# Six modulation steps of a hybrid attention block move from stage B to ahead of stage A, and their weights land in the heads' hl and pt tiles

## The chip, the core and the metric

The kernel runs on one core of one Trainium2 chip. The metric is device time in microseconds (us) of one execution, taken as the median of several runs. A core has five engines that run their own instruction streams and wait for each other through semaphores: PE (matrix multiply; its weight loads are listed as PEld), DVE (vector), ACT (scalar functions), POOL (general purpose) and SP, which here only starts DMA transfers. Each stream is in order: an instruction that waits holds up all that stand behind it on its engine. That holds for SP too, so a transfer whose buffer is not yet free keeps the later ones back.

## What is computed

The reference is a block of two layers on 512 latent tokens and 256 context tokens of width 1024. Cut to what matters:

```python
for l in range(2):
    sh, sc, gt = split(silu(c) @ w_ada[l] + b_ada[l], 3)              # and the same for c_ctx
    h  = rms_norm(x,   norm_g[l]) * (1 + sc)   + sh
    hc = rms_norm(ctx, norm_g[l]) * (1 + sc_c) + sh_c
    qa, ka, va, ga, qb, kb, vb, gb, qn, kn, vn, gn = split_proj(h @ w_in[l])     # and for hc
    ya = differential attention (4 heads, two softmaxes each)  * silu(ga)        # group A
    yb = grouped-query attention (6 heads, 2 key/value heads)  * silu(gb)        # group B
    yn = neighbourhood attention (6 heads, window, bias)       * silu(gn)        # group C
    y  = concatenate([ya, yb, yn]) @ w_out[l]
    x  = x + gt * y                                    # and ctx, in the first layer
```

The first line is the *modulation*: a product of two vectors with a matrix of 1024 x 3072 per layer. It gives a shift, a scale and an output gate for each of the 1024 features.

## The kernel before, in words

**Layout.** Activations lie with features on the 128 partitions. The input projection is cut into chunks of columns (`CH`): a0 and a1 hold keys, values and queries of group A, b0 and b1 those of B, c0, c1 and c2 those of C, and ga, gb, gn the gates. A chunk is 256 or 384 columns wide and is worked through in six tiles of 128 tokens (four of the latent stream, two of the context). A tile is 24 matmuls into one bank of PSUM: eight slices of features, three products each (the operands are split into a high and a low part, `mm3`, lines 679 to 681). Its weights come as raw float32 tiles by SP (line 76) and are split by ACT (line 89) and DVE or POOL (line 92). A raw buffer, of which there are three, is free for the next load when line 92 is done.

**Modulation.** The matrix is worked through in blocks of 128 columns, 24 per layer. One block is 512 KB, loaded in two halves of 256 KB. A *step* (`ada_step`, the generator `ada_blocks`) does one block: it starts the two loads of the block after it (line 227), does eight matmuls of 32 columns for its own (line 241; the profile counts sixteen, as each is two passes), copies the result on DVE (line 246), sums four strips with a selector matmul (line 248), and adds bias on DVE (line 251 or 254). The first call only loads. Blocks that layer 0 needs at its start are done earlier by `ada_pair` (line 204); the generator's list holds 32 more: the eight gate blocks of layer 0, sixteen of layer 1, and the eight gate blocks of layer 1.

**Order of the work.** After the a0 chunk (`proj_first`), seven calls of `ada_step` follow. Then come, layer by layer, the chunks a1 and ga (`F1`), stage A (heads of group A with the chunks b0, b1 and gb), stage B (heads of B with c0, c1, c2 and gn) and stage C. Within `proj` a step is put after every n-th tile; n is the cadence `st["cad"]`, set from the table `AK`: entry 0 is the number of steps right after a0, entry 1 the cadence in a1 and ga, entry 2 that in stage A (0: none), entry 3 that in stage B. In layer 0, a1 and ga have twelve tiles and stage B's chunks 24. This is the order in which the program is written; a scheduler then moves each instruction by priority (`prio` shifts it), by when its inputs are ready in its own model of time, and by when a buffer of the pool is free. So the instructions on an engine can stand in another order than in the code, and the steps right after a0 are spread over the tiles of a1.

**Buffers.** Tiles of one tag share a number of buffers; a new tile waits until the last reader of the one before it in that buffer is done. The tags here are `adw` (2 buffers of 2 KB per partition, for modulation weights), `hl` and `pt` (4 buffers of 3 KB each). In the stages of heads, `hl` takes the float16 high and low parts of a head's probabilities (ACT line 861, POOL line 862), and SP's transposing transfer (line 864) writes them to `pt`, from which PE does the pv matmuls (lines 897 and 898). Each is used for other things at other times: the modulation weights of the opening (`ada_load`), the six copies of a0's keys that are normalized and rotated (`qk_evac` with a tag; the last reader is DVE, line 506), and the part sums at the end of a layer. A step ahead of stage A takes its PSUM bank from `psV`, which the pv matmuls also use; a step in stage B takes it from `psP`, the two banks of the projection tiles.

The step takes its tile in these lines:

```python
def load(l, b):
    ts = []
    for r in range(2):
        t = sb([128, 512], F32, "adw", 2).rearrange("p (k n) -> p k n", n=128)
        SP.dma_start(out=t, in_=w_ada[l, b, :, 4 * r:4 * r + 4, :])
        ts.append(t)
    return ts
```

Of the kernel before, what the change touches and what calls it, by code (L numbers as in the profile page):

```python
# [10 lines left out]
F32 = mybir.dt.float32  # L11
# [30 lines left out]
}  # L42
REST = {"C": 7}
AK = [[6, 2, 0, 2], [0, 1, 0, 2]]
VSHARE = {"HA": (0, 1), "H": (0, 1), "G": (1, 1), "T": (1, 4), "HC": (1, 8), "WB": (1, 2), "WC": (1, 1),
          "W1": (1, 1)}

# [69 lines left out]
def tile_hybrid_block(ctx: ExitStack, tc: tile.TileContext, xT_d, cT_d, ng_d, w_ada, bT_d, w_in, w_out,  # L117
# [9 lines left out]
    share = Share(nc)  # L127

    def sb(shape, dt=F32, tag="", bufs=1):
        return pool.tile(shape, dt, tag=tag, bufs=bufs, name=tag)  # L130

    def prio(off):
        def deco(f):
            def g(*a, **k):
                tc.cur_priority += off
                try:
                    return f(*a, **k)
                finally:
                    tc.cur_priority -= off
            return g  # L140
        return deco
# [37 lines left out]
    def new_mods(l):  # L179
        mods[l] = (sb([128, KT, 2], F32, "mA", 2), sb([128, KT, 2], F32, "mB", 2), sb([128, KT, 2], F32, "mG", 2))  # L180
# [39 lines left out]
    def ada_blocks(blocks):  # L220


        def load(l, b):
            ts = []
            for r in range(2):
                t = sb([128, 512], F32, "adw", 2).rearrange("p (k n) -> p k n", n=128)
                SP.dma_start(out=t, in_=w_ada[l, b, :, 4 * r:4 * r + 4, :])
                ts.append(t)
            return ts

        nxt = load(*blocks[0])
        yield
        for i, (l, b) in enumerate(blocks):
            if l not in mods:
                new_mods(l)
            ts = nxt
            ps = (psV if share.phase == "1" else psP).tile([128, 512], F32, tag="pv" if share.phase == "1" else "p",
                                                           name="ada")
            for r in range(2):
                for g in range(4):  # L240
                    PE.matmul(ps[32 * g:32 * g + 32, 0:128], lhsT=cS[:, 4 * r + g, :], rhs=ts[r][:, g, :],
                              start=(r == 0), stop=(r == 1), tile_position=(0, 32 * g))
            if i + 1 < len(blocks):
                nxt = prio(-100)(load)(*blocks[i + 1])
            t = sb([128, 128], F32, "adt", 1)
            V.tensor_copy(t, ps[:, 0:128])
            src = ps[:, 128:130]
            PE.matmul(src, lhsT=t, rhs=sel, start=True, stop=True)
            w, kt = divmod(b, 8)
            if w == 1:  # L250
                V.tensor_scalar(out=mods[l][0][:, kt, :], in0=src, scalar1=bT1[:, l, kt:kt + 1],
                                scalar2=ng[:, l, kt:kt + 1], op0=ALU.add, op1=ALU.mult)
            else:
                V.tensor_scalar(out=mods[l][1 if w == 0 else 2][:, kt, :], in0=src, scalar1=bT[:, l, b:b + 1],
                                scalar2=None, op0=ALU.add)
            yield

    def ada_step():
        st["done"] = st.get("done", -1) + 1
        next(st["ada"], None)  # L260
# [22 lines left out]
    for l in range(DEPTH):  # L283
        for c in ORDER:
            n, c0 = CH[c][1], sum(v[1] for k, v in CH.items() if k < c)
# [747 lines left out]
    def run(gen):  # L1033
        for _ in gen:
            pass
# [5 lines left out]
    def fill(l, toks):  # L1041
        for c in toks:
            if c in CH:
                yield from proj(l, [c])
            elif c == "y":
                n = 6 if l == 0 else 4
                for j in range(0, n, 2):
                    y_pair(l, j)
                    yield
                    yield  # L1050
                for j in range(n):
                    if (l, "B", j) not in turned:
                        y_build(l, "gb", j)
                    yield
            elif c == "n":
                for db in range(KT):
                    while any((l, "C", j) not in turned for j in range(3)):
                        yield
                    out_head(l, db)
                    yield  # L1060
            else:
                yield from out_parts(l)
# [141 lines left out]
    if True:  # L1204
# [47 lines left out]
        proj_first(0, "a0", [[0, 1, 2, 3, 4, 5]], before0)  # L1252
        for _ in range(AK[0][0] + 1):
            ada_step()
        for l in range(DEPTH):
            share.phase = "1"
            st["cad"] = AK[l][1]
            run(fill(l, F1))
            st["cad"] = AK[l][2]
            both(l, "A", FA)  # L1260
            st["cad"] = AK[l][3]
            both(l, "B", FB)
# [108 lines left out]
```

## Time and profile before

| | us |
|---|---|
| median of 3 runs | 922.99 (919.12 to 923.62) |
| the profiled execution, its own time | 921.41 |
| its span in the trace | 919.6 |
| PE / DVE / ACT / POOL busy in the span | 824.1 / 681.9 / 593.1 / 544.1 |
| mean granted clock of PE | 0.957 |

The profile is one execution, recorded instruction by instruction. A row of the timeline gives start and length in us, the engine, the source line, the operation with the tiles it writes and reads, and in brackets the idle time of the engine ahead of it with what ended that. A row of the list of waits names who waited for whom, with the total in us, the number of times and the longest. A row of the stage table gives a stretch of time, its length, and for each engine the busy time with the number of instructions; behind them stand the granted clock of PE (1.00 is full speed), the mean share of the DMA engines that was busy, and GB/s.

### The profile page before, as it was taken

The numbers are of one execution on the slowest core, as the hardware profiler recorded it, in microseconds if no ns is written. First come the engines' busy times: TensorE is split into PE (matmuls) and PEld (weight loads), VectorE is DVE, ScalarE is ACT, GpSimd is POOL, SyncE is SP. The second block draws the span as 40 slices with busy tenths as digits, with TensorE's granted clock in tenths as the row PEclk, the third lists the DMA queues.
The fourth block names the chain that finished last, engine by engine and source line by source line (L and its number), as shares of the span: only waits on it lengthen the run. The fifth ranks groups of instructions, "written<-read, shape, count | busy, mean of one in ns | idle before, by whom it ended". The sixth has DMA issues, their size and how long they took to land. (4 is left out here: it accounts for less than half of the span.)

```text
span 919.6 us, 17947 instructions
## 1 busy us (share of the span) xinstructions
PE 824.1 (90%) x6386; PEld 705.7 (77%) x6386; DVE 681.9 (74%) x1306; ACT 593.1 (64%) x1269; POOL 544.1 (59%) x503
## 2 busy tenths in 40 slices
PE   6898988896998899896999989989959999987988
PEld 3687877795987688784778879978848878875667
DVE  4985787988778866557755798789977976876743
ACT  5334577785887687577663445478758888878630
POOL 1638855899698565434421036939988886654310
PEclk9999998998999999998999989999979999998999
DMA  9924895645879997998798723784547789999642
GB/s 325 320 88 127 202 198 151 139 102 136 190 156 212 223 213 178 223 262 217 145 232 245 246 76 92 173 206 98 123 131 188 133 199 255 205 233 250 129 87 88
DMA packets 307193, 165.46 MB, mean 180 GB/s; under 512 B 256544, under 2 KB 275232, under 8 KB 306976
## 3 DMA queue, kind: packets, MB, share of 16 engines
q1 hardware_dynamic: 307104, 164.33, 74.5%
q8 instruction: 50, 0.82, 0.4%
q14 instruction: 39, 0.32, 0.1%
HBM read 86.55 MB, written 15.47 MB: 111 GB/s over the span
## 5 line engine op out<-in xcount | busy, mean ns | idle before, releaser
L862 POOL TENSOR_TENSOR hl<-p,hl 128x768 f16<-128x768 f32 (+3 forms) x138 | 205.4, 1492 | 170.7 <-ACT hl L861 159.0
L679 PE MATMUL proj<-whi,bigL 128*128 128x384 f32 (+1 forms) x592 | 203.0, 344 | 8.5 <-DVE tb L602 5.1
L680 PE MATMUL proj<-wlo,bigL 128*128 128x384 f32 (+1 forms) x592 | 199.6, 337 | 0.8 <-POOL wlo L92 0.7
L681 PE MATMUL proj<-whi,bigL 128*128 128x384 f32 (+1 forms) x592 | 196.7, 334 | 0.0
L841 ACT ACTIVATE p<-sc,nb,gsc 128x768 f32<-128x768 f32 (+3 forms) x200 | 166.3, 845 | 10.9 <-DVE p L857 4.6
L827 DVE TENSOR_REDUCE mx<-sc 128x1 f32<-128x768 f32 (+2 forms) x128 | 118.6, 931 | 30.3 <-PE sc L775 30.3
L861 ACT CAST hl<-p 128x768 f16<-128x768 f32 (+3 forms) x144 | 104.4, 725 | 46.4 <-DMA pt<-hl 29.9
L679 PEld LDWEIGHTS proj<-whi,bigL 128*128 128x128 f32 x592 | 115.0, 194 | 18.9 <-DVE tb L602 7.2
L680 PEld LDWEIGHTS proj<-wlo,bigL 128*128 128x128 f32 x592 | 115.6, 195 | 3.9 <-POOL wlo L92 1.5
L681 PEld LDWEIGHTS proj<-whi,bigL 128*128 128x128 f32 x592 | 114.5, 194 | 2.7 <-issue 1.6
L92 POOL TENSOR_TENSOR wlo<-raw,whi 128x768 fp32r<-128x768 f32 (+1 forms) x44 | 82.8, 1889 | 31.7 <-ACT whi L89 28.1
L89 ACT CAST whi<-raw 128x768 fp32r<-128x768 f32 (+1 forms) x104 | 80.1, 779 | 25.3 <-DMA raw<-in_w_in_dram 11.1
L897 PEld LDWEIGHTS <-pt 128*128 128x128 f16 x736 | 66.4, 100 | 36.8 <-DMA pt<-hl 23.2
L679 PE MATMUL proj<-whi,bigC 128*128 128x384 f32 (+2 forms) x224 | 75.6, 337 | 1.0 <-ACT xn L462 1.0
L92 DVE TENSOR_TENSOR wlo<-raw,whi 128x768 fp32r<-128x768 f32 (+1 forms) x60 | 61.5, 1028 | 19.4 <-ACT whi L89 18.1
L680 PE MATMUL proj<-wlo,bigC 128*128 128x384 f32 (+2 forms) x224 | 74.3, 332 | 0.0
L163 POOL TENSOR_TENSOR rsqb<-rsqb,half 128x12 f32<-128x12 f32 (+2 forms) x25 | 68.5, 2739 | 9.7 <-DVE rsqb L162 8.8
L681 PE MATMUL proj<-whi,bigC 128*128 128x384 f32 (+2 forms) x224 | 73.6, 331 | 0.0
L898 PEld LDWEIGHTS <-pt 128*128 128x128 f16 x736 | 66.8, 100 | 4.6 <-issue 2.4
L775 PE MATMUL sc<-bigL 128*128 128x512 f16 (+4 forms) x184 | 46.5, 314 | 18.5 <-ACT p L841 18.1
L897 PE MATMUL pv<-vA,pt 128*128 128x128 f16 (+2 forms) x424 | 52.1, 230 | 12.1 <-DMA pt<-hl 12.1
L829 ACT ACTIVATE nb<-mx,lnp,gsc 128x1 f32<-128x1 f32 (+1 forms) x104 | 39.9, 385 | 33.3 <-DVE mx L827 22.5
(327 smaller groups left out, 2038.6 us busy)
## 6 DMA issues: line engine op xcount, KB each, us to landing
raw<-in_w_in_dram SPq DMA_DIRECT2D x64, 384.0 KB, 3.9
adw<-in_w_ada_dram SPq DMA_DIRECT2D x68, 256.0 KB, 3.5
raw<-in_w_out_dram SPq DMA_DIRECT2D x16, 384.0 KB, 4.5
raw<-in_w_in_dram SPq DMA_DIRECT2D x16, 256.0 KB, 3.0
g_d<-tb SPq DMA_DIRECT2D x20, 192.0 KB, 2.8
gt<-g_d SPq DMA_DIRECT2D x18, 192.0 KB, 3.6
hl<-in_w_ada_dram SPq DMA_DIRECT2D x12, 256.0 KB, 4.8
pt<-in_w_ada_dram SPq DMA_DIRECT2D x12, 256.0 KB, 4.9
```

The costliest lines, as they stand in the source:

```text
L89: self.nc.scalar.copy(out=hi, in_=raw2)
L92: self.share("W").tensor_tensor(out=lo, in0=raw2, in1=hi.bitcast(F32), op=ALU.subtract)
L163: G.tensor_tensor(out=y, in0=x, in1=half[:, 0:n], op=ALU.pow)
L679: PE.matmul(ps, lhsT=xh, rhs=hi, start=(kt == 0), stop=False)
L680: PE.matmul(ps, lhsT=xh, rhs=lo, start=False, stop=False)
L681: PE.matmul(ps, lhsT=xl, rhs=hi, start=False, stop=(kt == KT - 1))
L827: V.tensor_reduce(out=mx[:, 0:ns], in_=ps[:, 0:w * ns].rearrange("p (a b) -> p a b", b=w), axis=AX.X, op=ALU.max)
L841: A.activation(out=p[:, w * x:w * x + w], in_=u["ps", i][:, w * x:w * x + w], func=AF.Exp, bias=u["nb", i][:, x:x + 1], scale=lc[l]["sc"][ ...
L861: A.copy(out=hl[:, 0:n], in_=p)
L862: lo_eng.tensor_tensor(out=hl[:, n:2 * n], in0=p, in1=hl[:, 0:n], op=ALU.subtract)
L897: PE.matmul(po[r, :], lhsT=pt[:, b, r], rhs=V_[:, vt, c0:129], start=first, stop=False)
L898: PE.matmul(po[r, 0:65 - c0], lhsT=pt[:, nb + b, r], rhs=V_[:, vt, c0:65], start=False, stop=stop)
```

## The change

Two edits. The table `AK` for layer 0 goes from a step after every second tile of a1 and ga to one after every tile, and in stage B from every second tile to every fourth. So twelve steps in place of six are written into a1 and ga, and six in place of twelve into stage B; with the six after a0, 18 blocks in place of twelve are done ahead of stage A. The total stays. And while `share.phase` is "1", that is in the calls after a0 and in a1 and ga of both layers, a step's two halves are loaded into an `hl` and a `pt` tile in place of two `adw` tiles. In stage B they still go to `adw`. Layer 1's eight steps keep their place, and their loads move to the other tags with the same edit.

```diff
-AK = [[6, 2, 0, 2], [0, 1, 0, 2]]
+AK = [[6, 1, 0, 4], [0, 1, 0, 2]]
...
         def load(l, b):
             ts = []
             for r in range(2):
-                t = sb([128, 512], F32, "adw", 2).rearrange("p (k n) -> p k n", n=128)
+                if share.phase == "1":
+
+                    t = sb([128, 768], F32, *(("pt", 4) if r else ("hl", 4)))[:, 0:512]
+                else:
+                    t = sb([128, 512], F32, "adw", 2)
+                t = t.rearrange("p (k n) -> p k n", n=128)
                 SP.dma_start(out=t, in_=w_ada[l, b, :, 4 * r:4 * r + 4, :])
                 ts.append(t)
             return ts
```

Lines behind the edit are five higher in the changed kernel (227 becomes 232, 241 becomes 246, 679 becomes 684, 897 becomes 902). As each step loads for the one after it, the nineteenth block of the list is loaded ahead of stage A and used by the first step of stage B.

How the instructions move is read from the built programs. First SP's queue from the last raw loads of a0 to the first transposes of A's keys (`raw` are projection weights, `stg` the finished keys). Before:

```order
L76 DMA raw<-in_w_in_dram 128x768 x2
L227 DMA adw<-in_w_ada_dram 128x512 x2
L76 DMA raw<-in_w_in_dram 128x512 x4
L227 DMA adw<-in_w_ada_dram 128x512 x2
L76 DMA raw<-in_w_in_dram 128x512
L227 DMA adw<-in_w_ada_dram 128x512 x5
L534 DMA_TRANSPOSE bigL<-stg 128x8x128 x2
```

Changed:

```order
L76 DMA raw<-in_w_in_dram 128x768 x2
L232 DMA adw<-in_w_ada_dram 128x512 x2
L76 DMA raw<-in_w_in_dram 128x512 x5
L232 DMA pt<-in_w_ada_dram 128x512
L232 DMA hl<-in_w_ada_dram 128x512 x2
L232 DMA pt<-in_w_ada_dram 128x512
L232 DMA hl<-in_w_ada_dram 128x512
L232 DMA pt<-in_w_ada_dram 128x512 x2
L232 DMA hl<-in_w_ada_dram 128x512
L539 DMA_TRANSPOSE bigL<-stg 128x8x128 x2
```

The early `adw` pair carries the generator's first block before the change; now it carries stage B's first one that goes to `adw`, and the generator's first block is loaded into `hl` and `pt` behind the fifth raw load. The third step's pt half and the fourth's hl half go into buffers that a0's first two copies leave.

Second, PE at the end of a0 (`projs` and `proj` are projection banks, `cS` the two modulation vectors, `adt` the copy, `sel` the selector, `vb` a small sum for the scale of the values). Before:

```order
L680 MATMUL projs<-wlo,bigC 128x384
L681 MATMUL projs<-whi,bigC 128x384
L241 MATMUL ada<-adw,cS 32x128 x8
L248 MATMUL ada<-sel,adt 128x2
L241 MATMUL ada<-adw,cS 32x128 x4
L679 MATMUL proj<-whi,bigL 128x384
L680 MATMUL proj<-wlo,bigL 128x384
```

Changed, where the first step stands, 24 matmuls (one tile of a1) later:

```order
L685 MATMUL proj<-wlo,bigL 128x384
L686 MATMUL proj<-whi,bigL 128x384
L546 MATMUL vb<-vna_405,ones 128x1
L246 MATMUL ada<-hl,cS 32x128 x4
L246 MATMUL ada<-pt,cS 32x128 x4
L684 MATMUL proj<-whi,bigL 128x384
L685 MATMUL proj<-wlo,bigL 128x384
```

The first step moved behind the first tile of a1. The second stands 24 projection matmuls behind it, and the third 27 behind the second.

Third, PE at the first pv matmul, the first reader of a finished head (`sc` are scores). Before:

```order
L679 MATMUL proj<-whi,bigL 128x256
L680 MATMUL proj<-wlo,bigL 128x256
L681 MATMUL proj<-whi,bigL 128x256
L679 MATMUL proj<-whi,bigL 128x256
L897 LDWEIGHTS pt
L897 MATMUL pv<-vA,pt 128x128
```

Changed:

```order
L685 MATMUL proj<-wlo,bigC 128x256
L780 LDWEIGHTS bigL
L780 MATMUL sc<-bigL 128x512
L780 LDWEIGHTS bigL
L780 MATMUL sc<-bigC,bigL 128x256
L686 MATMUL proj<-whi,bigC 128x256
L902 LDWEIGHTS pt
L902 MATMUL pv<-vA,pt 128x128
```

Both stand behind 18 score matmuls. Ahead of it were 163 projection matmuls of width 256 (all of ga and 19 of b0) and the matmuls of twelve steps; now it is 264 of width 256 (ga and five tiles of b0) and the matmuls of 18 steps.

## The prediction

> **What bounds the kernel now.** I read the page's busy shares first, then the busy time by stage, then who PE waited for in the stages that the change touches, and last the rows of PE, SP and DVE around those waits.
>
> ```profile
> span 919.6 us, 17947 instructions
> PE 824.1 (90%) x6386; PEld 705.7 (77%) x6386; DVE 681.9 (74%) x1306; ACT 593.1 (64%) x1269; POOL 544.1 (59%) x503
> ```
>
> PE is busy for 90% of the span, so about 95 us of PE idle are all that a change without new arithmetic can win. The next rows split the part that matters here: the chunks a1 and ga ahead of stage A (from the end of a0 to the first pv matmul), layer 0's stage A, its stage B, and the like stretch of layer 1.
>
> ```profile
> 68.60:139.40 70.80, 64.88 (x542) 54.76 (x541) 51.32 (x122) 41.23 (x105) 50.36 (x49) 0.96 0.79 180
> 139.40:254.30 114.90, 100.37 (x727) 90.12 (x725) 96.74 (x147) 86.29 (x217) 93.46 (x96) 0.95 0.62 139
> 254.30:413.30 159.00, 149.28 (x1243) 128.11 (x1244) 110.17 (x218) 117.62 (x221) 97.22 (x72) 0.98 0.92 211
> 574.70:606.00 31.30, 30.02 (x285) 26.68 (x283) 23.17 (x47) 14.56 (x34) 27.69 (x27) 1.00 0.80 182
> ```
>
> After length, the columns are busy PE, PEld, DVE, ACT and POOL, each with its count, then granted clock, DMA share, GB/s. Stage B is PE's: 149.3 of 159.0 us. Stage A is shared: PE idles 14.5 us while DVE and POOL are busy for 97 and 93 of 115. Ahead of stage A PE idles 5.9 us, and the list of PE's waits between 62 and 140 us says for what: almost only for modulation weights.
>
> ```profile
> PE ada L241 <- DMA adw<-in_w_ada_dram: 5.4, 5, 2.0
> PE ada L248 <- DVE adt L246: 0.4, 1, 0.4
> ```
>
> PE's rows place two of these five waits; the clock was halved soon after both:
>
> ```profile
> 72.01 0.43 PE L241 MATMUL ada<-adw,cS 128*32 128x128 f32 x8 [1.97 <-DMA adw<-in_w_ada_dram]
> 135.96 0.43 PE L241 MATMUL ada<-adw,cS 128*32 128x128 f32 x8 [1.67 <-DMA adw<-in_w_ada_dram]
> 73.00:76.20 3.20, 3.20 (x12) 3.20 (x12) 1.88 (x6) 1.83 (x6) 3.20 (x5) 0.50 0.25 89
> 138.00:140.70 2.70, 2.70 (x15) 2.61 (x14) 1.09 (x3) 2.09 (x4) 0.73 (x1) 0.50 1.08 391
> ```
>
> At a granted clock of 0.50, 3.2 us of matmuls do the work of 1.6, and 2.7 us that of 1.4. So the two waits cost 3.0 us beyond themselves.
>
> The Trainium skill (TensorE: Matmul & The Clock Gate, Part 1: The HAM clock gate) says that the clock drops after an idle window of about 3.4 us. By that rule waits of 2 us would cost no clock; the trace disagrees, with 0.50 after 1.97 and after 1.67 us. With no clock loss in the terms below, the sum would be -3.0 in place of -4.4, and the time 920.0.
>
> **The change part by part.** *What a step costs PE.* A step puts two groups of ada matmuls and one selector pair between projection matmuls:
>
> ```profile
> 81.04 0.34 PE L681 MATMUL proj<-whi,bigL 128*128 128x384 f32 x1
> 83.12 0.34 PE L681 MATMUL proj<-whi,bigL 128*128 128x384 f32 x1
> 83.30 0.34 PE L679 MATMUL proj<-whi,bigL 128*128 128x384 f32 x1
> 83.56 0.43 PE L241 MATMUL ada<-adw,cS 128*32 128x128 f32 x8
> 83.92 0.45 PE L680 MATMUL proj<-wlo,bigL 128*128 128x384 f32 x1
> 87.18 0.34 PE L680 MATMUL proj<-wlo,bigL 128*128 128x384 f32 x1
> 87.36 0.28 PE L248 MATMUL ada<-sel,adt 128*128 128x2 f32 x2
> 87.50 0.42 PE L681 MATMUL proj<-whi,bigL 128*128 128x384 f32 x1
> ```
>
> Twelve projection matmuls start 2.08 us apart (81.04 to 83.12), 0.173 each. With a group between them the next starts 0.62 later, so a group costs 0.45; the selector pair makes 0.32 of 0.17, so 0.15. One step is 2 x 0.45 + 0.15 = 1.05 us. Six moved steps are 6.3 us of PE that go from stage B to the stretch ahead of A: nothing by themselves, as PE is the busy engine in both.
>
> *What goes ahead of stage A (layer 0).* With up to four tile pairs in place of one, a load is issued up to three steps ahead of its use, and the later steps find their weights there. I take all 5.8 us of waits and the 3.0 us of halved clock as gone: -8.8.
>
> *What comes in their place.* The first of these loads is now queued behind the fifth raw load of chunk a1, and until the six a0 copies in the hl and pt tiles are finished only one pair is free. The rows that set this:
>
> ```profile
> 68.34 0.34 PE L681 MATMUL projs<-whi,bigC 128*128 128x384 f32 x1
> 69.53 0.68 DVE L92 TENSOR_TENSOR wlo<-raw,whi 128x512 fp32r<-128x512 f32 x1
> 70.23 0.33 SPq L76 DMA_DIRECT2D raw<-in_w_in_dram  x1
> 84.27 0.68 DVE L506 TENSOR_TENSOR stg<-pt,stg 128x512 f16<-128x512 f32 x1
> L227 SPq DMA_DIRECT2D adw<-in_w_ada_dram x24: 327/372/1086, 69.1 to 137.1; - x24
> DMA to landing us min/median/max: 2.4/3.5/6.0
> ```
>
> The raw load starts when the split L92 has freed its buffer (70.21). The two ada loads follow at 70.56 and 70.93 (0.37 to issue one); the second lands 3.5 us on, at 74.4. PE ends a0 at 68.5, does one tile (24 x 0.173 = 4.2) and the small vb pair (0.2) and is there at 72.9: it waits 1.5. The second step's loads go out at about 75.1 into the same pair and are there by 79.0; PE comes at 79.4: no wait. The third step's pt tile is the one that L506 releases at 84.95, so its load lands at 88.4, and PE is there at about 84.6: it waits 3.8. From then on the copies release a tile every few microseconds and the lead grows. I take 5.3 us of waits, and one halved clock of 1.6, as after the 1.97: +6.9. The bounds are 1.5 (the release comes earlier; 3.8 and 1.6 vanish) and 13.5 (both loads take the longest landing, 6.0, so 2.5 more each, and both cost the clock).
>
> *Stage B loses six of its twelve steps.* There a step holds one of the two projection banks until DVE has copied and added, and PE waited at steps as follows (254 to 440 us):
>
> ```profile
> PE yt L640 <- DVE mB L254: 2.4, 1, 2.4
> PE ada L248 <- DVE adt L246: 1.7, 1, 1.7
> PE ada L248 <- DVE vnc L539: 1.5, 1, 1.5
> ```
>
> That is 5.6 us at twelve steps; half of it goes, -2.8, with bounds 0 and -5.6.
>
> *Layer 1's eight steps* also load into hl and pt now. PE's one wait there, between 573 and 612 us, goes: -0.7. Their number and place in the code stay.
>
> ```profile
> PE ada L241 <- DMA adw<-in_w_ada_dram: 0.7, 1, 0.7
> ```
>
> *The heads start later.* The cast of the first head needs an hl tile, which the last modulation loads now hold. Before, the first pv matmul came here:
>
> ```profile
> 117.27 0.28 PE L680 MATMUL proj<-wlo,bigL 128*128 128x256 f32 x1
> 117.63 0.28 PE L680 MATMUL proj<-wlo,bigL 128*128 128x256 f32 x1
> 139.44 0.33 PE L897 MATMUL pv<-vA,pt 128*128 128x128 f16 x1
> ```
>
> By the order of the built program, 163 matmuls of width 256 and 12 steps stand ahead of it before, 264 and 18 after, with 18 score matmuls in both. The 101 more cost 0.12 us each (0.36 for three), 11.9, and the steps 6.3: PE is 18.2 us of work ahead when the first pv comes, and that is 18.2 less the 1.9 us won (8.8 - 6.9), 16.3 us later: 155.7. Stages A and B then have the same heads and 18.2 us less of PE's other work. PE was 94% busy in B, DVE and ACT 69 and 74%; I take it that nearly all comes back and 1.0 us is lost in new waits for heads. The bounds are 0 and 18.2.
>
> *The held pair.* The nineteenth block is loaded ahead of stage A and used at B's first step, so one hl and one pt tile are out through stage A. ACT's waits for its cast into hl between 140 and 255 us (first row), and between 255 and 440 (second):
>
> ```profile
> ACT hl L861 <- DVE p L857: 8.7, 6, 4.3
> ACT hl L861 <- DMA pt<-hl: 8.3, 7, 3.6
> ```
>
> In A the cast never waited for a tile, in B it did for 8.3 us with four. I take 0 for three in A; the bound is 8.3 of ACT, in a stage where ACT has 29 us to spare.
>
> *Sum:* -8.8 + 6.9 - 2.8 - 0.7 + 1.0 = -4.4. The profiled execution took 921.4 us, 1.8 more than its span; -4.4 makes 917.0 of it. It lies 1.6 below the median of the runs, 923.0, so the median becomes 918.6. About 0.5%, 4.6 us, is what a measurement of this kernel can tell from no change, so the forecast is a gain at the edge of that.
>
> **The rivals.** *A larger gain:* the copy of a0 that the third step's load waits for is finished 4 us earlier, and the 3.8 and 1.6 fall away: -9.8, 913.2. For it: a built order in which the third step stands after only two tiles. Against: the copy goes through POOL first, which is busy throughout 77 to 82 us (the fifth column).
>
> ```profile
> 77.00:82.00 5.00, 5.00 (x42) 4.34 (x42) 2.38 (x13) 0.85 (x3) 5.00 (x6) 1.00 0.33 105
> ```
>
> *Nothing to measure:* both opening waits cost the clock (+1.6), and stage B's waits were DVE's lateness that the remaining steps meet as before (0 for -2.8): -4.4 + 1.6 + 2.8 = 0.0, 923.0. For it: the three waits at steps in B are single ones of twelve.
>
> *Slower:* from the first pv on, the heads are the bound. They start 16.3 us later, and the 18.2 us taken from PE come back only as far as DVE, ACT and POOL can run the heads faster. With two thirds lost, 12.1 for 1.0, the sum is +6.7: 929.7. It decides from 5.4 us lost on (slower than before) and shows from 10.0. For it: stage A's PE idle of 14.5 us, with DVE and POOL above 80%. Against: stage B, where PE is the one that is full, is longer.
>
> **How the numbers follow.** Forecast 0.40, its own range 915.5 to 921.5; larger gain 0.20; nothing 0.20; slower 0.20. Nearly half of the forecast, nearly all of the larger gain and some spread from the rest lie past -4.6 us: faster 0.41. Slower by more than 4.6: most of the slower case and a little of the others, 0.20. Within: 0.39. The range reaches from stage B's full 5.6 us on top of the larger gain, less some (908), to just past the slower case (931).
>
> **What would show it.** Right: no wait of PE for hl or pt loads after the fourth step ahead of A, one or two before it (72 to 75 and 85 to 89 us), granted clock of 1 near 138; the first pv at 155.7 (153 to 158); stage B's steps down to six and B shorter by 15 us or more. Wrong: PE waiting for ada loads all along the stretch; a first pv past 160; PE's waits for the heads' exp (L841) and their transposes growing by more than 6 us in A and B, which would be the slower case; ACT waiting for hl in stage A, which would be the held pair.

## The result, and the profile after

The changed kernel takes 931.55 us (median of 4 runs, 929.76 to 936.03); the kernel before, in runs on the same chip, 921.92. The medians differ by 9.6 us; the ratio over the runs (here and below it is an estimate of its own, not the quotient of the medians) is 1.0123, with a 95% interval of 1.0100 to 1.0147: slower, where 918.6 was forecast. The profiled execution took 929.76, 8.35 more than that of before.

The page of the changed kernel, first two lines:

```profile
span 928.0 us, 17959 instructions
PE 826.9 (89%) x6386; PEld 708.5 (76%) x6386; DVE 673.8 (73%) x1306; ACT 593.4 (64%) x1269; POOL 547.2 (59%) x503
```

PE's work is the same; its idle time and its halved clock grew. To see where, both traces are cut at the same pieces of work: at the start of the 145th, 433rd, 865th, 1440th and 1441st projection matmul. These are the end of a0; of a1 and ga; of b0, b1 and gb; of stage B's chunks; and the first of layer 1. Before, then the changed kernel (columns as in the stage table of the prediction):

```profile
72.40:133.00 60.60, 58.97 (x481) 50.36 (x478) 41.96 (x100) 34.21 (x88) 46.37 (x43) 0.97 0.77 176
133.00:244.90 111.90, 95.46 (x707) 85.06 (x705) 97.58 (x148) 81.71 (x200) 87.54 (x88) 0.94 0.62 136
244.90:413.00 168.10, 158.38 (x1299) 136.66 (x1298) 115.41 (x228) 125.35 (x244) 105.39 (x82) 0.98 0.92 212
413.00:535.40 122.40, 109.64 (x819) 88.14 (x819) 85.42 (x193) 66.17 (x142) 31.70 (x39) 0.95 0.84 215
535.40:919.60 384.20, 345.71 (x2595) 301.20 (x2595) 286.71 (x493) 254.76 (x525) 243.08 (x211) 0.95 0.69 156
```

```profile
70.60:131.80 61.20, 61.19 (x518) 53.73 (x519) 41.41 (x106) 32.53 (x84) 43.18 (x44) 0.97 0.89 222
131.80:237.60 105.80, 94.09 (x736) 82.59 (x735) 84.92 (x141) 72.79 (x169) 81.12 (x79) 0.98 0.62 147
237.60:414.70 177.10, 159.78 (x1264) 137.97 (x1262) 127.61 (x232) 137.74 (x281) 115.85 (x92) 0.96 0.81 184
414.70:542.00 127.30, 110.22 (x809) 89.66 (x808) 89.01 (x198) 67.68 (x146) 34.68 (x39) 0.92 0.82 211
542.00:928.00 386.00, 347.24 (x2595) 301.55 (x2595) 276.84 (x493) 253.31 (x525) 244.83 (x211) 0.95 0.68 156
```

The stretches differ by -1.8 (up to the 145th), +0.6, -6.1, +9.0, +4.9 and +1.8 us: 8.4 in all. At the end of stage A's chunks, the 865th projection matmul, the changed kernel is 7.3 us ahead, with six modulation steps more behind it and 48 pv matmuls fewer; stage B takes 9.0 back; the rest of layer 0 and layer 1 lose 6.7 more.

**Ahead of stage A the change did what it says.** PE's waits between 62 and 155 us, all of them:

```profile
PE proj L684 <- ACT pt L467: 2.1, 1, 2.1
PE proj L684 <- DVE vnb L547: 0.8, 1, 0.8
```

No wait for modulation weights is left, not even at the start. PE's rows show why, and where the first pv came:

```profile
70.61 0.45 PE L684 MATMUL proj<-whi,bigL 128*128 128x384 f32 x1 [2.15 <-ACT pt L467]
76.66 0.43 PE L246 MATMUL ada<-hl,cS 128*32 128x128 f32 x8
155.48 0.23 PE L902 MATMUL pv<-vA,pt 128*128 128x128 f16 x1
```

PE first waits 2.15 us for an a0 copy to leave its bank and then works at half clock (below), so it comes to the first step at 76.66; its weights had been there.

**The heads' first cast** is the row to look at next. ACT's rows before and after:

```profile
118.48 0.82 ACT L861 CAST hl<-p 128x768 f16<-128x768 f32 x1
```

```profile
144.68 0.83 ACT L866 CAST hl<-p 128x768 f16<-128x768 f32 x1 [0.56 <-PE ada L246]
```

It comes 26.2 us later, and what released it is the matmul of a modulation step: the four hl tiles were full of weights. ACT itself idles only 0.56 us for it; the rest of the delay lies in what stands ahead of the cast in ACT's order. The heads do not catch up: the 24th cast, counted in order of time, is still 22.8 us late. Before, then changed:

```profile
261.79 0.39 ACT L861 CAST hl<-p 128x256 f16<-128x256 f32 x1
```

```profile
284.64 0.41 ACT L866 CAST hl<-p 128x256 f16<-128x256 f32 x1
```

**In stage B** the heads of group A are still being finished. PE's waits between 248 and 415 us, the first three:

```profile
PE pv L902 <- DMA pt<-hl: 5.2, 5, 1.3
PE proj L684 <- DVE mB L259: 3.4, 1, 3.4
PE proj L684 <- DVE vA L591: 3.1, 1, 3.1
```

PE waits 3.45 us for a projection bank that a step holds, and DVE's rows show what stood ahead of the step's last operation (L259): the end of a head of group A (L929, which itself waited for POOL).

```profile
272.01 0.38 PE L253 MATMUL ada<-sel,adt 128*128 128x2 f32 x2 [0.66 <-DVE adt L251]
275.85 0.69 PE L684 MATMUL proj<-whi,bigL 128*128 128x384 f32 x1 [3.45 <-DVE mB L259]
```

```profile
272.34 0.68 DVE L832 TENSOR_REDUCE mx<-sc 128x2 f32<-128x512 f32 x1
273.60 2.00 DVE L929 TENSOR_TENSOR o<-tA,rA 128x256 f32<-128x256 f32 x1 [0.57 <-POOL rA L926]
275.52 0.14 DVE L544 TENSOR_REDUCE vnc<-vnc 128x1 f32<-128x4 f32 x1
275.59 0.20 DVE L259 TENSOR_SCALAR mB<-ada,bT 128x2 f32<-128x2 f32 x1
```

Both such waits came with a halved clock, as did the one at 70.6 (the stage table over those stretches):

```profile
272.50:279.30 6.80, 3.45 (x11) 3.46 (x12) 6.23 (x9) 6.47 (x18) 5.84 (x6) 0.51 0.59 149
293.00:299.80 6.80, 4.68 (x15) 4.69 (x16) 2.91 (x6) 4.96 (x8) 5.80 (x8) 0.51 0.99 211
71.10:74.50 3.40, 3.40 (x12) 3.40 (x12) 3.28 (x9) 3.18 (x12) 3.40 (x7) 0.51 0.65 222
```

**After stage B**, between 415 and 542 us, PE's longest waits are of other kinds, two of them for the heads' outputs that are turned (`yt`) for the output projection (`op`):

```profile
PE yt L645 <- DVE bigL L649: 3.9, 1, 3.9
...
PE op L1102 <- DVE bigL L628: 2.6, 1, 2.6
```

### The profile page after: what moved, and what is told of

It is laid out like the page before. It is cut to its first block, busy times and chain, and to the rows that moved or that the text cites. A ratio compares the mean times of both kernels' runs of the same rounds, so it can differ in the third digit from the quotient of the medians.

```text
span 928.0 us, 17959 instructions
## 1 busy us (share of the span) xinstructions
PE 826.9 (89%) x6386; PEld 708.5 (76%) x6386; DVE 673.8 (73%) x1306; ACT 593.4 (64%) x1269; POOL 547.2 (59%) x503
## 5 line engine op out<-in xcount | busy, mean ns | idle before, releaser
L867 POOL TENSOR_TENSOR hl<-p,hl 128x768 f16<-128x768 f32 (+3 forms) x138 | 207.8, 1510 | 157.3 <-ACT hl L866 147.9
L846 ACT ACTIVATE p<-sc,nb,gsc 128x768 f32<-128x768 f32 (+3 forms) x200 | 166.7, 844 | 27.3 <-POOL hl L867 12.1
L832 DVE TENSOR_REDUCE mx<-sc 128x1 f32<-128x768 f32 (+2 forms) x128 | 118.7, 930 | 29.0 <-PE sc L780 28.7
L866 ACT CAST hl<-p 128x768 f16<-128x768 f32 (+3 forms) x144 | 103.9, 725 | 33.1 <-DMA pt<-hl 26.2
L902 PEld LDWEIGHTS <-pt 128*128 128x128 f16 x736 | 67.6, 101 | 37.7 <-DMA pt<-hl 21.8
L163 POOL TENSOR_TENSOR rsqb<-rsqb,half 128x12 f32<-128x12 f32 (+2 forms) x25 | 69.3, 2771 | 10.5 <-DVE rsqb L162 5.7
L903 PEld LDWEIGHTS <-pt 128*128 128x128 f16 x736 | 67.6, 101 | 3.3 <-issue 1.0
L902 PE MATMUL pv<-vA,pt 128*128 128x128 f16 (+2 forms) x424 | 53.2, 232 | 12.7 <-DMA pt<-hl 12.1
L503 DVE TENSOR_TENSOR xn<-xn,rsqb 128x384 f32<-128x384 f32 (+1 forms) x44 | 50.3, 1170 | 14.9 <-POOL rsqb L163 10.5
```

The costliest lines, as they stand in the source:

```text
L163: G.tensor_tensor(out=y, in0=x, in1=half[:, 0:n], op=ALU.pow)
L832: V.tensor_reduce(out=mx[:, 0:ns], in_=ps[:, 0:w * ns].rearrange("p (a b) -> p a b", b=w), axis=AX.X, op=ALU.max)
L846: A.activation(out=p[:, w * x:w * x + w], in_=u["ps", i][:, w * x:w * x + w], func=AF.Exp, bias=u["nb", i][:, x:x + 1], scale=lc[l]["sc"][ ...
L866: A.copy(out=hl[:, 0:n], in_=p)
L867: lo_eng.tensor_tensor(out=hl[:, n:2 * n], in0=p, in1=hl[:, 0:n], op=ALU.subtract)
L902: PE.matmul(po[r, :], lhsT=pt[:, b, r], rhs=V_[:, vt, c0:129], start=first, stop=False)
```

## The experiments

All runs in one table, in us, each from its own trace: the start of the first cast; how many of the heads' casts had started when the 865th projection matmul did; the stretch from the 433rd to the 865th (A) and from there to the 1440th (B); from there to the first of layer 1 (C); layer 1 from then on; the ratio to the kernel before, with its interval. (The expectations count these marks 0.1 us later than the rows. Those that give layer 0, stage B or layer 1 as sums of stages, such as 516.0, 172 and 334.5 before, cut the trace where PE had done equal shares of its work instead; where a verdict needs these sums they are named so.)

| kernel | first cast | casts | A | B | A+B | C | layer 1 | ratio |
|---|---|---|---|---|---|---|---|---|
| before | 118.5 | 18 | 111.9 | 168.1 | 280.0 | 122.4 | 384.2 | |
| changed | 144.7 | 14 | 105.8 | 177.0 | 282.8 | 127.3 | 386.0 | 1.0123 (1.0100 to 1.0147) |
| cadence_only | 118.6 | 19 | 113.9 | 158.5 | 272.5 | 126.0 | 394.3 | 1.0070 (1.0037 to 1.0103) |
| tiles_only | 120.3 | 15 | 98.3 | 178.9 | 277.2 | 126.6 | 387.2 | 1.0007 (0.9983 to 1.0031) |
| tiles_first_eight | 119.2 | 19 | 119.5 | 154.0 | 273.5 | 128.2 | 400.1 | 1.0168 (1.0118 to 1.0219) |
| no_held_pair | 141.6 | 13 | 99.9 | 180.7 | 280.6 | 126.0 | 394.6 | 1.0170 (1.0132 to 1.0208) |
| sync_before | 118.9 | 18 | 109.7 | 169.7 | 279.4 | 127.9 | 388.0 | 1.0147 (1.0081 to 1.0214) |
| sync_after | 144.5 | 14 | 105.6 | 176.4 | 282.0 | 137.1 | 382.5 | 1.0156 (1.0106 to 1.0205) |
| sync_tiles | 119.5 | 15 | 98.5 | 177.4 | 275.9 | 131.5 | 383.2 | 1.0109 (1.0053 to 1.0165) |
| sync_cadence | 118.9 | 19 | 116.4 | 158.3 | 274.7 | 130.7 | 393.7 | 1.0162 (1.0109 to 1.0216) |
| both_in_pt | 120.3 | 15 | 108.0 | 172.6 | 280.6 | 126.4 | 380.5 | 1.0019 (0.9994 to 1.0045) |
| both_in_hl | 157.7 | 11 | 97.7 | 189.0 | 286.8 | 125.8 | 403.4 | 1.0325 (1.0291 to 1.0358) |
| third_adw_cadence | 119.5 | 17 | 108.2 | 163.0 | 271.2 | 130.8 | 389.6 | 1.0096 (1.0065 to 1.0127) |
| third_adw | 121.2 | 15 | 104.3 | 178.3 | 282.6 | 127.3 | 393.1 | 1.0146 (1.0102 to 1.0190) |
| hl_held | 139.7 | 13 | 101.4 | 181.7 | 283.1 | 121.9 | 385.6 | 1.0012 (0.9982 to 1.0042) |
| new_tiles_layer1 | 119.4 | 18 | 109.2 | 170.6 | 279.7 | 132.1 | 396.3 | 1.0235 (1.0200 to 1.0269) |
| cadence_tiles_layer1 | 118.7 | 19 | 116.4 | 157.7 | 274.1 | 133.6 | 396.5 | 1.0154 (1.0100 to 1.0208) |
| cadence_pt_layer1 | 118.4 | 19 | 119.2 | 158.1 | 277.4 | 146.2 | 379.2 | 1.0144 (1.0119 to 1.0169) |
| cadence_early_loads | 121.3 | 19 | 116.3 | 163.4 | 279.7 | 122.6 | 385.0 | 1.0021 (0.9999 to 1.0043) |
| cadence_6 | 118.9 | 19 | 118.7 | 152.4 | 271.1 | 132.8 | 382.4 | 0.9946 (0.9921 to 0.9971) |

A trace is one execution, and the sets of runs stand on different chips, on which the kernel before had medians of 920.38 to 923.20. A trace's time lies mostly within 4 us of the median of its kernel's runs, but sync_tiles' is 6.6 below, sync_before's 5.0 below, cadence_6's 5.4 above and hl_held's 4.3 above. So one pair of traces shows no difference under some 5 us; what repeats over several does.

### One part of the change alone

`cadence_only` has the new table and all loads in adw. `tiles_only` has the old table and the new tiles.

```diff
-AK = [[6, 2, 0, 2], [0, 1, 0, 2]]
+AK = [[6, 1, 0, 4], [0, 1, 0, 2]]
```

> The new table AK alone; all loads stay in the two adw tiles. Theory T (the tiles): weights in hl and pt keep the heads of group A from their own tiles, the heads run some 100 projection matmuls late through stage A and their last DVE work delays stage B's evictions. By T the heads are on time here (the 62nd pv matmul has 614 projection matmuls ahead of it, 552 before, 685 in the changed kernel), stage B loses nothing, and only waits for single-buffered weights are added, 13 of them ahead of A at up to 1.2 us and some halved clock: 918 to 928, B's waits for mB and vA absent. Theory C (the cadence: PE's work that was moved leaves stage B without filling): 929 to 933, as the changed kernel or a little worse.

> The new tiles alone; AK as before, so every second tile has a step. Theory T: the first pv matmul stays at 451 projection matmuls, but the 123rd comes at 758 in place of 721 and the 184th at 912 in place of 860, about half of the changed kernel's lateness: slower than before by 2 to 6 us, 924 to 928, and PE waits for DVE at the start of stage B. Theory C: the 5.8 us of waits for weights and 3 us of halved clock ahead of A go, nothing is lost: 913 to 918.

`tiles_first_eight` and `no_held_pair` are the changed kernel with one condition more:

```diff
-                if share.phase == "1":
+                if share.phase == "1" and l == 0:          # tiles_first_eight
+                if share.phase == "1" and st["done"] != 18:  # no_held_pair
```

> The changed kernel, but only the generator's first eight blocks (those of layer 0) go to hl and pt, all later ones to adw. Theory T: the tiles are free again when the heads want them; 601 projection matmuls ahead of the 62nd pv and 706 ahead of the 123rd (685 and 834 in the changed kernel): no loss in stage B, a few waits for adw in the last ten steps ahead of A; 914 to 922. Theory C: as the changed kernel, 929 to 933.

> The changed kernel, but the nineteenth block, which waits through stage A for stage B's first step, goes to adw. Theory T: the heads are as late as in the changed kernel (676 projection matmuls ahead of the 62nd pv, 851 ahead of the 123rd; 685 and 834 there), since they start late and not because a pair is missing: 927 to 933. Theory P (the held pair: with three of four tiles the heads' casts and transposes wait in A): the loss goes, 914 to 921.

Measured: 927.24, 920.94, 934.90 and 936.22 us (before 921.73). By totals theory T missed three of the four: tiles_only cost nothing, tiles_first_eight was among the slowest, and no_held_pair lay above its range too. The totals mix two things, which the table takes apart. In layer 0 the first cast is late only where cadence and late blocks in the tiles come together, in the changed kernel and in no_held_pair:

```profile
118.63 0.82 ACT L861 CAST hl<-p 128x768 f16<-128x768 f32 x1
```

```profile
141.59 0.83 ACT L866 CAST hl<-p 128x768 f16<-128x768 f32 x1 [0.88 <-PE ada L246]
```

(cadence_only, then no_held_pair). A+B is 272.5 and 273.5 with the new cadence and the cast on time, 282.8 and 280.6 with it late. Theory P falls: without the held pair the cast is still late, and stage B as long (180.7). Theory C falls for layer 0: with PE's steps moved, cadence_only's stage B is 9.6 us *shorter* than before, of which six steps fewer at 1.05 us make 6.3. So the moved steps cost A+B only where the heads are late as well: with the cast on time the new cadence takes 7.5 us off (280.0 to 272.5), with the new tiles it adds 5.6 (277.2 to 282.8). tiles_only's 15 casts are no sign of late heads: its first 24 casts come 1.5 us earlier on average than before, and PE is at the 865th matmul 14.6 us earlier. But cadence_only loses 3.6 us in C and 10.1 in layer 1, tiles_first_eight 15.9 in layer 1, where nothing of the work was changed. That made a new theory, S, the subject of the next four runs.

### Layer 1 from the same state

One line brings all engines together between the layers, in the kernel before, the changed one, tiles_only and cadence_only:

```diff
+            tc.strict_bb_all_engine_barrier()
             x = [big(0), big(1)]
             open_norm()
```

> The kernel before, with all engines brought together once between layer 0 and layer 1, so that layer 1 starts from the same state in this run and in the next three. It gives the base for them. Theory S (the whole program is ordered anew, and layer 1, whose code is not changed, got a worse order in every variant so far: 54.8 + 106.9 + 98.9 + 73.7 us before, 10.7 to 15.5 more in three of five variants): with the order of layer 1 changed here too, this kernel is slower than before by 4 to 15 us, more than the few us that bringing the engines together costs. Theory L (the layer 1 losses come from layer 0's change itself): slower by 0 to 4.

> The changed kernel with the same meeting of the engines. Layer 0 was 6.8 us longer in the changed kernel's trace than before (522.8 to 516.0 us of its stages). Theory T (late heads in layer 0): 4 to 9 us above sync_tiles, which has the same order in layer 1; stage B of layer 0 about 181 us.

> The new tiles with the old cadence, with the meeting. Its ACT and POOL order in layer 1 is word for word that of sync_after, DVE's and SP's all but a few rows: by theory S layer 1 takes the same time in both within 2 us, and the two differ by layer 0 alone, 4 to 9 us in favour of this one. If layer 1 differs by more with the same order, S is wrong and chance in the runs (the clock) is as large as these effects.

> The new cadence with adw tiles, with the meeting. Layer 0 was 5.6 us shorter than before in its trace (510.4 to 516.0), layer 1 10.7 longer. Theory S: with layer 1 started from the same state the loss in layer 1 against sync_before goes or shrinks to 3 us, and this kernel is the fastest of the four, 2 to 6 us below sync_before. Theory L: it is 4 to 7 us above sync_before, as without the meeting.

Medians: 934.93, 936.13, 930.90 and 936.29 (before 923.20). sync_before is 11.7 us above before, in the range of S; how much of that is the meeting itself these runs don't tell. Layer 1 of sync_after and of sync_tiles, which have the same order there, instruction by instruction on PE, DVE, ACT and POOL:

```profile
551.50:934.00 382.50, 349.90 (x2595) 304.50 (x2595) 283.52 (x493) 252.67 (x525) 243.56 (x211) 0.94 0.68 157
```

```profile
539.30:922.50 383.20, 344.70 (x2595) 298.86 (x2595) 282.82 (x493) 252.38 (x525) 244.40 (x211) 0.97 0.69 157
```

382.5 and 383.2: as S says. Their totals differ by 5.2, within the 4 to 9 expected, though the intervals overlap. sync_cadence fits neither S nor L: it is 1.4 above sync_before, its layer 1 still 5.7 longer, in an order that is not the same (at the same place in the order stand 86% of POOL's rows and 64% of ACT's). The pair sync_before and sync_cadence, 279.4 and 274.7, and the pair sync_tiles and sync_after, 275.9 and 282.0, repeat in A+B what was found without the meeting.

### Which tile, and a third buffer

`both_in_pt` and `both_in_hl` are the changed kernel with both halves of a block in one kind of tile; `third_adw_cadence` and `third_adw` have three adw buffers (lines 188 and 226) and no hl or pt tiles, with the new and the old table.

```diff
-                    t = sb([128, 768], F32, *(("pt", 4) if r else ("hl", 4)))[:, 0:512]
+                    t = sb([128, 768], F32, "pt", 4)[:, 0:512]   # both_in_hl: "hl"
```

```diff
-                t = sb([128, 512], F32, "adw", 2)
+                t = sb([128, 512], F32, "adw", 3)
```

> The changed kernel with both halves of a modulation block in pt tiles and none in hl. Theory T2 (the loss of layer 0 is the first cast of the heads, which waits until the steps give an hl tile back; it came at 144.8 in the changed kernel, at 118.6 to 120.4 where cadence or tiles were changed alone): the first cast comes at 117 to 122, layer 0's four stages take 508 to 517 us (522.6 in the changed kernel, 515.9 before), stage B 166 to 174; the whole is 2 to 10 us below the changed kernel unless layer 1 gets a worse order. Theory C (PE's moved work leaves stage B empty whatever the heads do): layer 0 at 520 or more.

> The mirror: both halves in hl tiles, none in pt. Theory T2: the first cast at 144 or later, layer 0 at 521 to 535, stage B over 178; the slowest of this call. Theory C: as both_in_pt, as cadence and number of loads are the same.

> The new cadence, no hl or pt tiles, but three adw buffers in place of two. Theory T2: heads on time (first cast 118 to 121), fewer waits for weights ahead of stage A than with two (5.1 us of idle above 0.45 us there): layer 0 at 506 to 513, 3 to 10 us under before. The total is this plus what the order of layer 1 brings, 333 to 350 us in the traces so far (334.5 before): 912 to 930. Theory C: layer 0 at 520 or more.

> The kernel before with three adw buffers alone. Layer 0: 0 to 5 us under before (part of the 5.8 us of waits for weights ahead of A). Layer 1 by theory S (any edit re-deals its order, and the order before is better than most): 336 to 346 against 334.5, though nothing of its code changed but the buffer; total 918 to 930. If layer 1 stays at 333 to 335, the losses of layer 1 are not a matter of order alone.

Medians: 922.45, 951.83, 930.76 and 936.52 (before 920.38). The first cast obeys T2:

```profile
120.35 0.83 ACT L866 CAST hl<-p 128x768 f16<-128x768 f32 x1
```

```profile
157.67 1.57 ACT L866 CAST hl<-p 128x768 f16<-128x768 f32 x2
```

With the same cadence and the same loads, both_in_hl has 11 casts done and A+B of 286.8, both_in_pt 15 and 280.6: theory C, which wants them alike, falls here too. But T2's numbers for both_in_pt missed (cut by PE's work, layer 0 takes 518.8 and stage B 176.5; both_in_hl has 523.8 and 185.1, as expected): its transposes now want the pt tiles (one, at line 869, waits 2.9 us on SP for the selector matmul of a step), so the heads fall behind a little later: the fifth to the 24th cast come 14.2 us late on average. The first cast alone does not tell it. third_adw is the plainest case for S: one more buffer, and 16 us slower by the medians (ratio 1.0146), above the 918 to 930 expected. In its trace layer 1 makes 8.9 of it, C 4.9 and A+B 2.6; its layer 0 was expected shorter and was not. Nor was that of third_adw_cadence as short as expected (515.9 by PE's work, for 506 to 513), and its total lies just above its range.

### Late heads alone, and layer 1 alone

`hl_held` is the kernel before; idle tiles hold hl until the twelfth step is copied:

```diff
+            if l == 0:
+                st["held"] = [sb([128, 768], F32, "hl", 4) for _ in range(4)]
+                for h in st["held"]:
+                    G.memset(h[:, 0:1], 0.0)
...
             V.tensor_copy(t, ps[:, 0:128])
+            for h in (st["held"] if i == 11 else []):
+                V.tensor_tensor(out=sb([128, 1], F32, "keep", 1), in0=h[:, 0:1], in1=t[:, 0:1], op=ALU.add)
```

> The kernel before, with the four hl tiles taken by idle tiles from the end of a0 until the twelfth step ahead of stage A has been copied (about 136 us); no transfer, no cadence and no matmul is changed, only four memsets on POOL and four small adds on DVE are added. Theory T2 (the first cast is what counts): the first cast at 137 to 146, as in the changed kernel, in place of 118.6; at the 865th projection matmul 14 or 15 casts are done in place of 18; from there to the 1440th 174 to 182 us in place of 168.1; layer 1's first projection matmul 3 to 10 us later than 535.5. Rival C (it is the moved work or the transfers): layer 1's first projection matmul at 533 to 538.

`new_tiles_layer1` is the kernel before with the condition `l == 1 and b >= 16` for the new tiles; `cadence_tiles_layer1` has the new table too; `cadence_pt_layer1` puts both halves in pt.

> The kernel before, with hl and pt tiles for the last eight blocks only, those of layer 1. Layer 0 is ordered as before up to its last stage: layer 1's first projection matmul at 534 to 538. Layer 1's order is, on ACT and POOL word for word, that of no_held_pair, which took 394.5 us from there to the end (384.1 before, 385.9 in the changed kernel, whose loads in layer 1 go to the same tiles): theory S gives 391 to 398 and a total of 927 to 937. If it is the tiles that matter in layer 1 and not the order: 384 to 388, total 919 to 926.

> The new cadence with adw tiles in layer 0 and hl and pt tiles for the last eight blocks. Layer 0 as in cadence_only: layer 1's first projection matmul at 529 to 533, before 535.5. Layer 1 in yet another order, 380 to 403 in the traces so far with these tiles: total 911 to 937; faster than both kernels if the order is one of the better half.

> As the run before it, but both halves of the last eight blocks in pt tiles, as in both_in_pt, whose layer 1 was the shortest (380.4). Layer 0: first projection matmul of layer 1 at 529 to 533. Total 911 to 930.

Medians: 922.62, 943.50, 935.51 and 934.54 (before 920.97). hl_held's first cast and its stage B:

```profile
139.65 1.56 ACT L863 CAST hl<-p 128x768 f16<-128x768 f32 x2
```

```profile
235.90:417.60 181.70, 164.98 (x1356) 141.11 (x1354) 128.92 (x248) 136.27 (x284) 114.19 (x92) 0.96 0.90 203
```

With cadence, transfers and matmuls as before, late casts make stage A 10.5 us shorter and stage B 13.6 longer, the picture of the changed kernel: A+B +3.1, the first of layer 1 +4.1, as T2 says (13 casts are done, one less than it gave). The total, 1.0012 (0.9982 to 1.0042), can't be told from before; its trace is the longest of its ten executions. So with the old cadence late casts alone cost at most 0.4%.

Layer 1 of no_held_pair and of new_tiles_layer1, the same order on ACT and POOL behind different layers 0:

```profile
538.90:933.50 394.60, 348.29 (x2595) 303.16 (x2595) 287.83 (x493) 253.04 (x525) 245.49 (x211) 0.95 0.67 152
```

```profile
547.20:943.50 396.30, 351.20 (x2595) 305.96 (x2595) 288.11 (x494) 253.17 (x525) 245.46 (x211) 0.94 0.68 152
```

394.6 and 396.3, where the tiles alone would have given 384 to 388: S again. Late heads are no rival here: in all twenty traces the first cast of layer 1 comes 73.5 to 77.2 us after its first projection matmul. Nor does the kind of tile explain the spread: in the ten kernels that load layer 1's blocks to adw, layer 1 takes 382.4 to 400.1. Whether it adds to it (380.5 and 379.2 with pt alone, 403.4 with hl alone) stays open. new_tiles_layer1, cadence_tiles_layer1 and cadence_pt_layer1 all missed the mark expected for the first of layer 1: it came at 547.2, 539.8 and 555.4, since C took 132.1, 133.6 and 146.2. So the first's total lay above its range, and the two others lost in C, cadence_tiles_layer1 in layer 1 too (396.5), what A and B had won; cadence_pt_layer1, with a layer 1 of 379.2, missed its range too.

### An order near that of before

`cadence_early_loads` and `cadence_6` are cadence_only with one number changed each:

```diff
-                nxt = prio(-100)(load)(*blocks[i + 1])
+                nxt = prio(-200)(load)(*blocks[i + 1])
```

```diff
-AK = [[6, 1, 0, 4], [0, 1, 0, 2]]
+AK = [[6, 1, 0, 6], [0, 1, 0, 2]]
```

> The new cadence with adw tiles, the loads' priority at -200 in place of -100. Layer 1's order is the nearest to before of 25 tried (on POOL 95% of its rows stand as before, on ACT 76%; 83 and 66% in cadence_only). Theory S: the 1440th projection matmul at 403 to 408 (413.1 before), layer 1 from its first projection matmul on 382 to 389 us, total 912 to 921. Rival (layer 1 loses with the cadence, not with the order): layer 1 at 391 to 397, total 923 to 930.

> The new cadence ahead of stage A and every sixth tile in place of every fourth in stage B, so that two of its six steps come at its end; adw tiles. POOL's order in layer 1 is to 93% that of before, ACT's to 73%. Theory S: the 1440th projection matmul at 403 to 409, layer 1 384 to 392, total 914 to 925. Rival: layer 1 at 391 to 397, total 924 to 931.

Medians 923.30 and 915.53 (before 921.54). cadence_early_loads got layer 1 as S says (385.0), but its 1440th projection matmul came at 414.5, not at 403 to 408: the same edit changed the order of stages A and B too (A+B 279.7, for 272.5 in cadence_only), and the total fell to the rival's range. cadence_6 is faster than both kernels, 0.9946 (0.9921 to 0.9971), with its total and its 1440th projection matmul (403.9) in S's ranges and layer 1 below its. Its stage B and its layer 1:

```profile
251.60:403.90 152.30, 145.38 (x1116) 128.35 (x1115) 116.70 (x194) 116.49 (x224) 103.90 (x77) 0.99 0.84 194
...
536.70:919.10 382.40, 346.21 (x2595) 299.98 (x2595) 288.79 (x494) 254.06 (x526) 243.76 (x211) 0.96 0.69 157
```

## Why the prediction was wrong, step by step

**The waits ahead of stage A** (-8.8, +6.9) were mis-sized to the safe side. Neither of the two opening waits came: PE waited 2.15 us for an a0 copy, ran 3.4 us at half clock, and reached the first step 3.8 us later than the working had it; the copy that the third load waits for was done at 82.8, 2 us earlier than the working had it (DVE's row):

```profile
82.10 0.72 DVE L511 TENSOR_TENSOR stg<-pt,stg 128x512 f16<-128x512 f32 x1
```

From the 145th to the 433rd projection matmul PE is busy for 61.19 of 61.20 us. In the terms of the sum, the stretch up to the first pv has 2.9 us of waits and 1.7 of halved clock (half of the 3.4) in place of the 6.9: -4.2, between the forecast's -1.9 and the larger-gain rival's -7.3. The 7.3 us by which PE is ahead at the end of stage A's chunks is another measure, as its work up to there is not the same.

**The steps in stage B** (-2.8): their waits did not shrink. Of the 5.6 us in the working, 2.4 lie behind stage B's chunks, at a matmul that belongs to no step:

```profile
418.04 1.12 PE L640 MATMUL yt<-ident,xn 128*128 128x128 f32 x4 [2.43 <-DVE mB L254]
```

So 3.2 us at twelve steps became 4.5 at six, 3.4 of it at one of them and with a halved clock; DVE's rows above put that one down to late heads.

**The heads start later** (+1.0) is the step that failed. The first pv came at 155.48, for 155.7 forecast, and that looked like the mark of the delay. It is not: cadence_only's first pv came still later, at 168.18 (its row follows), and its stage B is the shortest but one in the first six rows of the table.

```profile
168.18 0.23 PE L897 MATMUL pv<-vA,pt 128*128 128x128 f16 x1
```

What counts is the chain ahead of pv, cast, subtraction and transpose, on ACT, POOL and SP. The prediction saw that the first cast needs a tile that the weights hold, but priced it as PE work that had gone ahead of the first pv. The cast was 26.2 us late, and the heads did not catch up in stage A. The table's count of casts puts stage B in order: 152 to 163 us with 19 casts done, 168 to 171 with 18, 163 with 17, 173 to 179 with 15, 176 and 177 with 14, 181 and 182 with 13, 189 with 11; all kernels with 19, and the one with 17, have the new cadence, with 6.3 us less of steps in B. Most of it is a shift between A and B, and the count also falls where PE is early, as in tiles_only.

The delay of the casts themselves tells the two apart. Against before, the first 24 casts are late on average by 12.1 us in both_in_pt, by 19.9 to 20.4 in the changed kernel, no_held_pair, sync_after and hl_held, and by 35.2 in both_in_hl; by 6.6 in third_adw; and by -1.9 to 3.7 in all others. A+B in us, by cadence:

| | heads on time | heads late by 12 us or more |
|---|---|---|
| new cadence | 271.1 to 279.7 (8 kernels) | 280.6 to 286.8 (5 kernels) |
| old cadence | 275.9 to 280.0 (5 kernels) | 283.1 (hl_held) |

third_adw, late by 6.6, has 282.6. In pairs it is 10.3 us between the changed kernel and cadence_only, where the prediction had 1.0 for the late heads; 6.2 between both_in_hl and both_in_pt; and 3.1 between hl_held and before. The eight on time differ by 8.6 among themselves, so the size of the loss is less sure than its direction.

The slower rival had the right direction, with 12.1 lost, and its 929.7 lies 1.9 from the median; but the first pv, its condition, was the wrong one, and much of the loss in the trace stands in C and layer 1, so that its number came so near is luck. (In the working, 101 matmuls at 0.12 us make 12.1 and not 11.9; nothing hangs on it.)

**The held pair** (0): removing it left the cast at 141.6 and A+B 2.2 shorter; 0 stands within what a pair of traces shows.

**Layer 1** (-0.7) took +1.8, and C, which had no term, +4.9. This is the second thing that failed, an assumption that the sum never named: that work whose code is not touched keeps its time. The whole program is ordered anew at each edit. C and layer 1 together took 506.6 us before; in the 15 other traces without the meeting of the engines they took 506.9 to 530.1, and only both_in_pt, hl_held and cadence_early_loads came within 1 us of before. The order goes with the time: two pairs of kernels with the same order in layer 1 agree within 0.7 and 1.7 us, kernels with the same instructions and other orders spread from 379 to 403, those with adw tiles in layer 1 from 382 to 400.

The clock rule of the Trainium skill (TensorE: Matmul & The Clock Gate, Part 1: The HAM clock gate), an idle window of about 3.4 us, disagrees with this trace as well: the wait at 70.61 was 2.15 us, and the clock stood at 0.51 from 71.1 to 74.5.

**What stays open.** How the 9.6 us divide between late heads and the new order can't be told: in the trace +1.7 had gathered at the 1440th projection matmul and +6.7 behind it, but hl_held alone is not measurably slower in total. Why the orders of C and layer 1 differ in time was not followed wait by wait.

## What to carry to other kernels

Before an idle tile is lent, ask who takes it next and how long that chain is: a load that sits in it may cost nothing itself and still start another engine's work late. Look for the first instruction of the waiting chain, not for the one on the bound engine. Where a scheduler orders the whole program, an edit is also a new deal for all that is not edited, here worth -2 to +16 us in layer 1 where neither its cadence nor its kind of tile was changed, up to more than the whole loss of the changed kernel; compare stages at equal work, and try neighbours of a good edit before dropping it.

## What the runs showed that was not expected

The granted clock falls in stretches of 3.4 us or twice that (71.1 to 74.5, 272.5 to 279.3, 293.0 to 299.8), around waits of 2.15, 3.45 and 3.1 us. PE was busy for 3.40, 3.45 and 4.68 us in these stretches, so the half clock cost about 1.7, 1.7 and 2.3 us beyond the waits. Not every such wait has this price: in the changed kernel the clock stayed at 1.00 around a wait of 2.33 us (PE's row, then the stage table).

```profile
392.98 0.72 PE L780 MATMUL sc<-bigC 128*128 128x256 f16 x5 [2.33 <-DMA bigC<-stg]
390.60:399.00 8.40, 6.07 (x48) 4.88 (x46) 2.92 (x5) 5.39 (x13) 2.57 (x3) 1.00 1.21 255
```

And executions of one kernel spread more than these effects: the kernel before took 914.56 to 926.13 in 19 runs, so only medians and intervals carry a verdict at 1%.
